# A hybrid DeltaNet / sparse-attention layer: constants loaded first, gate rows kept in DRAM, and the last down-projection unit swept token tile by token tile

## The chip, the cores and the metric

The kernel runs on one core of one Trainium2 chip. The metric is the device time of one execution in microseconds (us). The kernel before takes 3674.93 us, the median of three runs (3673.78, 3674.93, 3680.48). Its profile comes from one further execution, which took 3680.55 us.

## The reference, cut to what matters

One inference step of a one-layer decoder on a prompt of 2048 tokens and on 8 single-token samples, all in float32, width 1024, feed-forward width 2816:

```python
mod = silu(c) @ w_ada + b_ada                  # six parts of 1024: shift, scale, gate, twice
h = rmsnorm(x, g_norm) * (1 + scale1) + shift1
p = h @ w_in                                   # columns for both head groups
o = concat(gated_deltanet(p), sparse_attention(p))
x = x + gate1 * (o @ w_out)
h = rmsnorm(x, g_norm2) * (1 + scale2) + shift2
a = silu(h @ w1) * (h @ w3)                    # w_ffn_in
x = x + gate2 * (a @ w_ffn_out)
y = rmsnorm(x, g_final)
```

The names in this excerpt are shortened; the outputs also hold the new keys, values, indexer keys, convolution rows and DeltaNet states. What the change touches is `mod`, the two gated additions, and the last line.

## The kernel before, in words

**Arithmetic.** A float32 product is made from three passes of TensorE: both operands are split into a rounded high part and a rest, and `mm3` (lines 178 to 182) issues high by high, high by low, low by high. Every 128x512 weight tile is therefore cast on ACT (L163) and subtracted on DVE (L164) before TensorE can use it.

**Stages.** The prompt is worked in 4 groups (g = 0 to 3) of 512 tokens, each of 4 token tiles (t = 0 to 3) of 128. First come the constants (L245 to L291), the modulation (L294 to L367) and, group by group, the normalisation of the input, the projections `w_in` and the DeltaNet chain. The second stage runs the sparse attention (index scores L1626, softmax, `PT` x `V` at L1688), the eight samples, and per group `ffn(g)` (L1751 to L1994): `w_out`, a gated addition, the second normalisation, `w_ffn_in` in 11 pairs, two pairs to a unit (the last unit has one pair), and after each unit's pairs its share of `w_ffn_out`, here called the down projection, in two column halves `hf`. A last unit has two weight tiles per half. The sums of one half stand in the four PSUM banks `d`, one for each token tile.

**The start.** SyncE (SP) issues nearly all loads from one queue, in program order. The vectors come first, then parts 0 and 1 of `w_ada`, eight 512 KB pieces each, into tiles that are borrowed from later work (hh, hl, qk, kq, ct, wi; L314 to L316), then the rest of the constants `cf` (L329) and `cr` (L330), then the first group's input `xt` (2 MB, `load_x`, L435 and L626), then the weights `wsr` and `wr` of `w_in`. `modulate(part)` takes 512 columns at a time: 8 products of a `w_ada` tile with the conditioning (L351), a copy out of PSUM on ACT (L353), then 16 small products with the selection matrix `f4` (L358), which is part of `cf`, and the addition of the bias on DVE (L360). `xt` is squared on ACT (L375). The first product of the projections is L180 with the normalised input `hh` (cast at L414).

**Gate rows.** The two gated additions need the gate along the free axis, the same in all partitions. `rowb(base)` (L1728 to L1739) makes it: for each half 4 transposes of a broadcast column of `mod` (L1735, base 16 or 40) into a `g` bank, and one ACT copy (L1737). It is called twice in each group, before `w_out` and before `w_ffn_in`. The tile `row` has two buffers, and `g_final` is loaded into one of them too (L1983).

**The gated addition.** `gated_add` (L1766) multiplies a bank by `row` on DVE (L1769) into `tm` for t < 2 and into `ca` for t >= 2, and adds the product to `xt` (L1770), on DVE where its argument `soon` is set, else on GpSimd (POOL). Only the second half of the last unit has `soon` in the down projection.

**The order of the work.** Several generators run in turns under a planner (`weave`, `step`, L491 to L529). Each yields an estimated TensorE time, waits and the PSUM tags that it uses or needs. The planner keeps a model of when a PSUM slot comes free and switches to attention pieces whenever their share is due. So the order of the instructions is fixed when the program is built, and a yield that goes missing shifts which attention piece falls beside which part of `ffn`. The tag `g` is shared by `rowb` and the attention output.

**The end.** In the last group the samples' part of each weight tile (16 products with 32 columns, L1812) is issued beside the prompt's. After the last unit the queue of side work is emptied (`tick(True)`, L1981), `g_final` is loaded, and each token tile is closed: `rnorm` (L382 on DVE, the power on POOL at L383), the scaling (L1986, DVE), the output DMA (L1987). The samples' row comes last (L1993, L1994). A second copy of attention and feed-forward stands behind a branch at L1543 that this input doesn't take.

Of the kernel before, what the change touches and what calls it, by code (L numbers as in the profile page):

```python
# [25 lines left out]
F32 = mybir.dt.float32  # L26
# [10 lines left out]
D = 1024  # L37
# [18 lines left out]
RB = 2  # L56
# [56 lines left out]
class K:  # L113
# [102 lines left out]
    def build(self):  # L216
        tc, nc = self.tc, self.nc
        with ExitStack() as es:
# [12 lines left out]
            self.vp_d = self.dr.tile([NS, 128, NPAGE, 256], F32, name="vp_d")  # L231
            self.x2_d = self.dr.tile([T, D], F32, name="x2_d")
# [61 lines left out]
    def modulation(self):  # L294
# [18 lines left out]
        self.ada = [st[i::2] for i in range(2)]  # L313
        for part in range(2):  # L314
            for k in range(KB):
                nc.sync.dma_start(self.ada[part][k], A["w_ada"][0, k * 128:(k + 1) * 128, part * D:(part + 1) * D])  # L316
# [12 lines left out]
        nc.sync.dma_start(self.cf[:, 128:], A["cf"][:, 128:NC0])  # L329
# [100 lines left out]
    def phase1(self, es):  # L430
# [4 lines left out]
        self.x0 = self.load_x(0)  # L435
# [145 lines left out]
    def projects(self):  # L581
        nxt = None
        for g in range(self.ng):
# [15 lines left out]
            for said in extra:  # L599
                yield said[0], said[1]  # L600
        yield lambda: not self.queue
# [1126 lines left out]
    def rowb(self, base):  # L1728

        nc, p = self.nc, self.p  # L1730
        row = p.tile([128, D], F32, name="row", tag="row", bufs=RB)
        for a in range(2):
            pt = self.ps.tile([128, 512], F32, name="g", tag="g", bufs=2)
            for k in range(4):
                self.o(nc.tensor.transpose(pt[:, k * 128:(k + 1) * 128],  # L1735
                                    self.mod[:, base + a * 4 + k, 0:1].to_broadcast([128, 128]), self.id))
            nc.scalar.copy(row[:, a * 512:(a + 1) * 512], pt)  # L1737
            yield TP, 0, dict(act=0.6, use="g", need=None if a else "g")
        return row  # L1739
# [11 lines left out]
    def ffn(self, g):  # L1751
# [8 lines left out]
        def P(tag):  # L1760
            return self.ps.tile([128, 512], F32, name=tag, tag=tag, bufs=2)
# [53 lines left out]
        def after(gap, cost, run):  # L1815
            side.append((gap, run, cost))
# [23 lines left out]
        yield 0, 0, dict(need="g")  # L1840
        row = yield from self.rowb(16)
# [32 lines left out]
        yield 0, 0, dict(need="g")  # L1874
        row = yield from self.rowb(40)
# [10 lines left out]
        if samp:  # L1886
# [16 lines left out]
            after(1, 0, lambda: None)  # L1903
        np_ = FF // 256
        ms = self.msq()
        per = 2
        for p0 in range(0, np_, per):
# [52 lines left out]
            for hf in range(2):  # L1960
                cs = slice(hf * 512, (hf + 1) * 512)
                pd = D4()
                pq = P("g") if samp else None
                for b in range(nf):
                    fr = (p0 * 2 + b) * 128
                    wh, wl, wr = weights([A["w_ffn_out"][0, fr:fr + 128, cs]])
                    if samp:
                        beside(pq, ax[:, b, :], wr, b == 0, b == nf - 1)
                    yield from three(pd, lambda t: ah[b][:, S(t)], lambda t: al[b][:, S(t)], wh, wl, b, nf - 1)
                last = p0 + per >= np_  # L1970
                for t in range(4):
                    gated_add(pd[t], row[:, cs], xt[:, t, cs], last and hf, t)
                    if last:
                        self.squares(ms[:, t, hf:hf + 1], xt[:, t, cs])
                if samp:
# [6 lines left out]
        gf = p.tile([128, D], F32, name="row", tag="row", bufs=RB)  # L1982
        nc.sync.dma_start(gf, bass.AP(tensor=A["g_final"].tensor, offset=A["g_final"].offset, ap=[[0, 128], [1, D]]))  # L1983
        for t in range(4):
            r = self.rnorm(ms[:, t:t + 1])
            nc.vector.scalar_tensor_tensor(xt[:, t, :], xt[:, t, :], r, gf, op0=OP.mult, op1=OP.mult)  # L1986
            nc.sync.dma_start(O[0][0, g * GT + t * 128:g * GT + (t + 1) * 128], xt[:, t, :])  # L1987
        if samp:
            r = mean(ms)
            gv = gf.rearrange("p (h j c) -> p h j c", h=2, j=4)  # L1990
# [27 lines left out]
```

## Time and profile before

| | |
|---|---|
| median of three runs | 3674.93 us |
| profiled execution | 3680.55 us, span 3678.6 us |
| mean granted clock of TensorE | 0.965 |
| PE (matmul), PEld (weight load) | 3429.4 us (93%), 2649.0 us (72%) |
| DVE, ACT, POOL | 2090.6 us (57%), 1475.8 us (40%), 599.2 us (16%) |
| read from and written to HBM | 435.49 MB, 124.75 MB |

The profiled execution is 5.6 us above the median and beside the slowest of the three runs. A row of the timeline gives the start, the duration, the engine, the line, the operation with output and input tiles, and in brackets how long the engine had stood idle and what released it. A row of the chain of waits gives the start, the length and the work that the end was waiting for then. In the windows view each row is a stretch of time with the busy time of each engine, the granted clock of TensorE (PEclk), the share of the DMA engines and GB/s.

### The profile page before, as it was taken

Reading aid. Unit: us, or ns where it says so; the run is one execution under the profiler, and the core shown is the slowest. Engines: PE = TensorE matmul, PEld = TensorE weight load, DVE = VectorE, ACT = ScalarE, POOL = GpSimd, SP = SyncE. Lnnn points to the kernel's source line nnn. Section 1 sums busy time; section 2 is a strip of 40 time slices with the busy share of each in tenths; the row PEclk is TensorE's granted clock in tenths of the full one; section 3 lists DMA queues with packets and bytes.
Section 4 is the critical chain, followed back from the end, with each engine's and each line's share of the span. In section 5 each row is a group of like instructions: output and inputs, shape, how many; then the busy total and the mean of one; then the engine's idle time right before and its main releaser. Section 6 shows DMA issues by size and latency. Waiting matters only on the chain.

```text
span 3678.6 us, 62998 instructions
## 1 busy us (share of the span) xinstructions
PE 3429.4 (93%) x23441; PEld 2649.0 (72%) x23441; DVE 2090.6 (57%) x4377; ACT 1475.8 (40%) x2868; POOL 599.2 (16%) x548
## 2 busy tenths in 40 slices
PE   7999999999998898999888999999899999899997
PEld 5867778777776776777665677787677777677775
DVE  3656646646644665666667555667666664443434
ACT  3333323323334333344456544564645543322222
POOL 0001000101001023212210122212022112221213
PEclk7999999999999898999998999999999999899998
DMA  6755575575676225455544453335433233432221
GB/s 246 244 204 164 180 243 175 184 241 167 193 262 205 70 94 157 124 167 161 158 153 130 127 174 113 114 98 177 138 91 99 90 103 107 169 107 80 78 82 64
DMA packets 412270, 545.52 MB, mean 148 GB/s; under 512 B 47364, under 2 KB 285225, under 8 KB 411946
## 3 DMA queue, kind: packets, MB, share of 16 engines
q1 hardware_dynamic: 411954, 541.41, 46.2%
q8 instruction: 186, 3.05, 0.3%
q14 instruction: 130, 1.06, 0.1%
HBM read 435.49 MB, written 124.75 MB: 152 GB/s over the span
## 4 chain that ended last, share of the span: by engine, by line
PE 74%; DVE 9%; DMA 7%; ACT 4%; issue 4%; SPq 1%; POOL 0%; DVEq 0%; ACTq 0%; POOLq 0%
PE d L180 18%; PE d L182 16%; PE d L181 16%; PE s L1626 3%; PE g L1688 3%; PE s L1671 2%; DVE wi L164 1%; PE g L1700 1%; DMA wi<-kept 1%; PE g L1812 1%; DMA wr<-in_w_ffn_out_dram 1%; DMA x_d<-xt 1%; PE g L1058 1%; ACT bias L1500 1%; ACT wi L163 1%
## 5 line engine op out<-in xcount | busy, mean ns | idle before, releaser
L180 PE MATMUL d<-hh,wi 128*128 128x512 f32 x1792 | 778.8, 435 | 24.0 <-DVE tm L1769 5.8
L181 PE MATMUL d<-hl,wi 128*128 128x512 f32 x1792 | 710.6, 397 | 7.0 <-DVE hl L415 5.8
L182 PE MATMUL d<-hh,wi 128*128 128x512 f32 x1792 | 710.6, 397 | 0.0
L164 DVE TENSOR_TENSOR wi<-wr,wi 128x512 fp32r<-128x512 f32 x537 | 402.7, 750 | 470.1 <-ACT wi L163 467.4
L163 ACT CAST wi<-wr 128x512 fp32r<-128x512 f32 x537 | 332.3, 619 | 784.5 <-PE d L182 499.2
L180 PEld LDWEIGHTS d<-hh,wi 128*128 128x128 f32 x1792 | 342.0, 191 | 120.9 <-issue 29.4
L182 PEld LDWEIGHTS d<-hh,wi 128*128 128x128 f32 x1792 | 341.6, 191 | 77.8 <-DVE wi L164 0.8
L181 PEld LDWEIGHTS d<-hl,wi 128*128 128x128 f32 x1792 | 343.1, 191 | 75.6 <-DVE hl L415 10.6
L180 PE MATMUL d<-wi,hh 128*128 128x512 f32 x768 | 324.7, 423 | 20.5 <-DMA wi<-kept 13.2
L180 PE MATMUL d<-wi,ah 128*128 128x512 f32 x704 | 301.2, 428 | 8.8 <-ACT ah L1940 5.6
L181 PE MATMUL d<-wi,hh 128*128 128x512 f32 x768 | 302.0, 393 | 1.0 <-DVE wi L164 1.0
L182 PE MATMUL d<-wi,hl 128*128 128x512 f32 x768 | 302.4, 394 | 0.0
L182 PE MATMUL d<-wi,al 128*128 128x512 f32 x704 | 282.2, 401 | 3.2 <-POOL al L1941 2.6
L181 PE MATMUL d<-wi,ah 128*128 128x512 f32 x704 | 282.2, 401 | 0.0
L1941 POOL TENSOR_TENSOR al<-ca,ah 128x512 fp32r<-128x512 f32 x88 | 119.1, 1365 | 844.9 <-ACT ah L1940 608.4
L1635 DVE SCALAR_TENSOR_TENSOR sc<-rl,iw,sc 128x512 f32<-128x512 f32 (+3 forms) x224 | 165.8, 740 | 81.5 <-ACT rl L1628 75.5
L1628 ACT ACTIVATE rl<-s 128x512 f32<-128x512 f32 (+3 forms) x288 | 150.3, 544 | 144.1 <-PE s L1626 136.6
L1770 POOL TENSOR_TENSOR xt<-xt,tm 128x512 f32<-128x512 f32 x96 | 136.5, 1436 | 411.5 <-DVE tm L1769 365.7
L180 PEld LDWEIGHTS d<-wi,hh 128*128 128x128 f32 x768 | 145.2, 189 | 68.7 <-DMA wi<-kept 17.0
L1626 PE MATMUL s<-ik,iqT 128*128 128x512 f32 (+3 forms) x576 | 170.8, 396 | 10.0 <-ACT rl L1628 9.7
L1500 ACT ACTIVATE bias<-sc,sv 128x640 bf16<-128x640 f32 (+11 forms) x120 | 169.7, 1414 | 22.8 <-DVE sv L1502 13.5
L180 PEld LDWEIGHTS d<-wi,ah 128*128 128x128 f32 x704 | 135.2, 192 | 52.6 <-issue 11.0
(532 smaller groups left out, 5587.5 us busy)
## 6 DMA issues: line engine op xcount, KB each, us to landing
wi<-kept SPq DMA_DIRECT2D x168, 512.0 KB, 3.4
wr<-in_w_ffn_in_dram SPq DMA_DIRECT2D x572, 128.0 KB, 2.3
wr<-in_w_ffn_out_dram SPq DMA_DIRECT2D x143, 256.0 KB, 2.6
kept<-wi SPq DMA_DIRECT2D x56, 512.0 KB, 3.4
xt<-in_x_prompt_dram SPq DMA_DIRECT2D x8, 2048.0 KB
row<-in_w_ada_dram SPq DMA_DIRECT2D x32, 512.0 KB, 4.3
wr<-in_w_in_dram SPq DMA_DIRECT2D x56, 256.0 KB, 3.6
kT<-kT_d SPq DMA_DIRECT2D x54, 256.0 KB, 3.0
```

The costliest lines, as they stand in the source:

```text
L163: nc.scalar.copy(w[:, 0], wr)
L164: nc.vector.tensor_tensor(w[:, 1], wr, w[:, 0].bitcast(F32), op=OP.subtract)
L180: self.o(nc.tensor.matmul(out, wh, xh, start=start, stop=False, **kw))
L181: self.o(nc.tensor.matmul(out, wh, xl, start=False, stop=False, **kw))
L182: self.o(nc.tensor.matmul(out, wl, xh, start=False, stop=stop, **kw))
L1500: nc.scalar.activation(c, s, AF.Sign, bias=t, accum_out=cnt)
L1626: self.o(nc.tensor.matmul(ps[:, :w], iq[:, h, :].bitcast(F32R), B["ikT"][c * 2 + a][:, :w].bitcast(F32R), start=a == 0, stop=a == 1))
L1628: nc.scalar.activation(r[:, :w], ps[:, :w], AF.Relu)
L1635: nc.vector.scalar_tensor_tensor(s, r[:, :w], iw, s, op0=OP.mult, op1=OP.add)
L1688: self.o(nc.tensor.matmul(po[:, :256], V[:, kb % 4, :], PT[:, b * 256:(b + 1) * 256], start=kb == 0, stop=kb == i))
L1770: (nc.vector if soon else nc.gpsimd).tensor_tensor(xt, xt, tm, op=OP.add)
L1941: nc.gpsimd.tensor_tensor(al[b], a, ah[b].bitcast(F32), op=OP.subtract)
```

## The change

Three parts, independent in the text:

1. The load of `cf` is issued ahead of `w_ada`, and the load of the first group's `xt` between `w_ada` part 0 and part 1. `cr` keeps its place behind part 1.
2. The gate column of `mod` is copied on DVE after projections g = 1 (base 16) and g = 3 (base 40) and written to DRAM, 1024 elements of 4 bytes. `rowb` is then one DMA that reads this row into all partitions (512 KB), on SP's queue. Its transposes, its ACT copies and its three kinds of yields are gone.
3. The second half of the last group's last down unit keeps both weight tiles and sweeps t by t: all six products of a token tile, then its gated addition, its squares and its close. In all groups the close stands in the loop over the token tiles, and `g_final` is loaded by the first close.

```diff
+        nc.sync.dma_start(self.cf[:, 128:], A["cf"][:, 128:NC0])
         for part in range(2):
+            if part:
+                self.x0 = self.load_x(0)
             for k in range(KB):
                 nc.sync.dma_start(self.ada[part][k], A["w_ada"][0, k * 128:(k + 1) * 128, part * D:(part + 1) * D])
...
-        nc.sync.dma_start(self.cf[:, 128:], A["cf"][:, 128:NC0])
         nc.sync.dma_start(self.cr, A["cf"][:, NC0:])
...
-        self.x0 = self.load_x(0)
...
+            for base in {1: (16,), 3: (40,)}.get(g, ()):
+                nc = self.nc
+                col = self.m("gate")
+                nc.vector.tensor_copy(col[:, 0:8], self.mod[:, base:base + 8, 0])
+                nc.sync.dma_start(self.gates[base].rearrange("(m c) -> c m", c=128), col[:, 0:8])
...
     def rowb(self, base):
-        for a in range(2):
-            pt = self.ps.tile([128, 512], F32, name="g", tag="g", bufs=2)
-            for k in range(4):
-                self.o(nc.tensor.transpose(pt[:, k * 128:(k + 1) * 128],
-                                    self.mod[:, base + a * 4 + k, 0:1].to_broadcast([128, 128]), self.id))
-            nc.scalar.copy(row[:, a * 512:(a + 1) * 512], pt)
-            yield TP, 0, dict(act=0.6, use="g", need=None if a else "g")
+        row = self.p.tile([128, D], F32, name="row", tag="row", bufs=RB)
+        g = self.gates[base]
+        self.nc.sync.dma_start(row, bass.AP(tensor=g.tensor, offset=g.offset, ap=[[0, 128], [1, D]]))
         return row
...
-        yield 0, 0, dict(need="g")
-        row = yield from self.rowb(16)
+        row = self.rowb(16)
...
+        def close(t):
+            if not gf:
+                gf.append(p.tile([128, D], F32, name="row", tag="row", bufs=RB))
+                nc.sync.dma_start(gf[0], bass.AP(tensor=A["g_final"].tensor, offset=A["g_final"].offset, ap=[[0, 128], [1, D]]))
+            r = self.rnorm(ms[:, t:t + 1])
+            nc.vector.scalar_tensor_tensor(xt[:, t, :], xt[:, t, :], r, gf[0], op0=OP.mult, op1=OP.mult)
+            nc.sync.dma_start(O[0][0, g * GT + t * 128:g * GT + (t + 1) * 128], xt[:, t, :])
+
+        def finish(t, pd):
+            cs = slice(512, 1024)
+            gated_add(pd, row[:, cs], xt[:, t, cs], True, t)
+            self.squares(ms[:, t, 1:2], xt[:, t, cs])
+            close(t)
...
+                    if samp and hf and last:
+                        kept.append((wh, wl))
+                    else:
+                        yield from three(pd, lambda t: ah[b][:, S(t)], lambda t: al[b][:, S(t)], wh, wl, b, nf - 1)
+                for t in range(4 if kept else 0):
+                    for b, w in enumerate(kept):
+                        self.mm3(pd[t], ah[b][:, S(t)], al[b][:, S(t)], *w, b == 0, b == nf - 1)
+                        yield 3 * MM, 0, bank(t, b, nf - 1)
+                    finish(t, pd[t])
+                if kept:
+                    self.done += nf
+                for t in range(0 if kept else 4):
                     gated_add(pd[t], row[:, cs], xt[:, t, cs], last and hf, t)
                     if last:
                         self.squares(ms[:, t, hf:hf + 1], xt[:, t, cs])
+                    if last and hf:
+                        close(t)
```

**What moves at the start.** SP's queue at the start of the program, before: the second part of `w_ada` (hl to wi), then the constants, then the input of group 0 (xt).

```order
L316 DMA hl<-in_w_ada_dram 128x1024 x4
L316 DMA qk<-in_w_ada_dram 128x1024
L316 DMA kq<-in_w_ada_dram 128x1024
L316 DMA ct<-in_w_ada_dram 128x1024
L316 DMA wi<-in_w_ada_dram 128x1024
L329 DMA cf<-in_cf_dram 128x482
L330 DMA cr<-in_cf_dram 128x1224
L626 DMA xt<-in_x_prompt_dram 128x4x1024
L442 DMA al<-in_a_log_dram 128x4
```

The same queue now, from the constants on to the second part of `w_ada`:

```order
L315 DMA cf<-in_cf_dram 128x482
L320 DMA hh<-in_w_ada_dram 128x1024 x4
L320 DMA qk<-in_w_ada_dram 128x1024
L320 DMA kq<-in_w_ada_dram 128x1024
L320 DMA ct<-in_w_ada_dram 128x1024
L320 DMA wi<-in_w_ada_dram 128x1024
L633 DMA xt<-in_x_prompt_dram 128x4x1024
L320 DMA hl<-in_w_ada_dram 128x1024 x4
```

`cf` has moved ahead of sixteen pieces, and `xt` ahead of eight of them; what follows `cr` keeps its order.

ACT's queue at the same place, before: squares of `xt` (L375), casts of the first input weights (L163) and the copies out of the modulation's banks (L353; 257 and 264 are those of part 1's first half, 281 and 288 those of its second).

```order
L163 CAST wi<-wr 128x512
L375 ACTIVATE junk,msq<-xt 128x512
L163 CAST wi<-wr 128x512
L375 ACTIVATE junk,msq<-xt 128x512
L353 COPY m_257<-s 128x512
L375 ACTIVATE junk,msq<-xt 128x512
L353 COPY m_264<-s 128x512
L375 ACTIVATE junk,msq<-row 8x512 x2
L353 COPY m_281<-s 128x512
L353 COPY m_288<-s 128x512
L163 CAST wi<-wr 128x512
```

Now, with the same copies under the numbers 259, 266, 283 and 290:

```order
L378 ACTIVATE junk,msq<-xt 128x512 x5
L356 COPY m_259<-s 128x512
L356 COPY m_266<-s 128x512
L447 ACTIVATE nA<-al 128x4
L459 CAST wsh<-wsr 128x320 x2
L378 ACTIVATE junk,msq<-row 8x512 x2
L163 CAST wi<-wr 128x512
L356 COPY m_283<-s 128x512
L163 CAST wi<-wr 128x512
L356 COPY m_290<-s 128x512
L854 COPY raw<-hist 128x3 x4
L163 CAST wi<-wr 128x512
```

All squares of `xt` now precede part 1's first copies, and two casts of input weights stand ahead of its last copy.

**What moves between group 0 and group 1.** TensorE's queue behind the last down product of group 0, before (L1626 index scores, L1671 attention scores; ik numbers name key blocks):

```order
L182 MATMUL d<-wi,al 128x512
L1626 MATMUL s<-ik_15047,iqT 128x512
L1626 MATMUL s<-ik_15049,iqT 128x512
L1671 MATMUL s<-kT,qT 128x512
L1626 MATMUL s<-ik_15047,iqT 128x512
L1626 MATMUL s<-ik_15049,iqT 128x512
L1626 MATMUL s<-ik_15051,iqT 128x128
L1626 MATMUL s<-ik_15053,iqT 128x128
```

The same place now (L1633 is the old L1626, L1707 the old L1700 that transposes probabilities, L1695 the old L1688):

```order
L182 MATMUL d<-wi,al 128x512
L1707 MATMUL g<-cf,big 128x128 x4
L1695 MATMUL g<-PT,V 128x256 x2
L1633 MATMUL s<-ik_15047,iqT 128x512
L1633 MATMUL s<-ik_15049,iqT 128x512
L1707 MATMUL g<-cf,big 128x128 x4
L1695 MATMUL g<-PT,V 128x256 x2
L1633 MATMUL s<-ik_15047,iqT 128x512
L1633 MATMUL s<-ik_15049,iqT 128x512
L1633 MATMUL s<-ik_15051,iqT 128x512
```

An earlier piece of attention now falls behind the last down product: from there to the first `w_out` product of group 1 the queue holds 88 products, where it held 56 with the 8 transposes of `rowb`. Among the last 48 down products of group 0 stand 18 attention products now, 54 before.

**What moves at the end.** DVE's queue in the last unit of group 3, before (banks 36107 to 36110 are t = 0 to 3 of the second half):

```order
L1769 TENSOR_TENSOR tm_36092<-d_36040,row_32582 128x512
L1769 TENSOR_TENSOR ca_36169<-d_36109,row_32582 128x512
L1769 TENSOR_TENSOR ca_36174<-d_36110,row_32582 128x512
L1770 TENSOR_TENSOR xt_32128<-xt_32128,ca_36169 128x512
L1769 TENSOR_TENSOR tm_36154<-g_36043,sc_32153 128x128
L1769 TENSOR_TENSOR tm_36159<-d_36107,row_32582 128x512
L1770 TENSOR_TENSOR xt_32128<-xt_32128,ca_36174 128x512
L1541 TENSOR_SCALAR again_36241<-g_36239 1x1
L1769 TENSOR_TENSOR tm_36164<-d_36108,row_32582 128x512
L1770 TENSOR_TENSOR xt_32128<-xt_32128,tm_36159 128x512
L1770 TENSOR_TENSOR xt_32128<-xt_32128,tm_36164 128x512
L1769 TENSOR_TENSOR tm_36187<-g_36111,sc_32153 128x128
```

The same place now (banks 36027 to 36030 are t = 0 to 3; L1770 and L1771 are the old L1769 and L1770):

```order
L1770 TENSOR_TENSOR tm_36012<-d_35960,row_32513 128x512
L1770 TENSOR_TENSOR tm_36048<-d_36027,row_32513 128x512
L1771 TENSOR_TENSOR xt_32070<-xt_32070,tm_36048 128x512
L1770 TENSOR_TENSOR tm_36067<-d_36028,row_32513 128x512
L1771 TENSOR_TENSOR xt_32070<-xt_32070,tm_36067 128x512
L1770 TENSOR_TENSOR ca_36084<-d_36029,row_32513 128x512
L1771 TENSOR_TENSOR xt_32070<-xt_32070,ca_36084 128x512
L1770 TENSOR_TENSOR ca_36101<-d_36030,row_32513 128x512
L1770 TENSOR_TENSOR tm_36120<-g_35963,sc_32084 128x128
L1771 TENSOR_TENSOR xt_32070<-xt_32070,ca_36101 128x512
L1770 TENSOR_TENSOR tm_36133<-g_36031,sc_32084 128x128
L385 SCALAR_TENSOR_TENSOR rny4_36055<-msq_32536 128x1
```

The token tiles are now taken in the order 0, 1, 2, 3, each multiplied and added before the next; before, tiles 2 and 3 came first. The closes follow behind all four, as before.

More of the change, by code (lines that the diff above doesn't have):

```diff
@@ L231, in build @@
             self.vp_d = self.dr.tile([NS, 128, NPAGE, 256], F32, name="vp_d")
+            self.gates = {b: self.dr.tile([D], F32, name=f"gate{b}") for b in (16, 40)}
             self.x2_d = self.dr.tile([T, D], F32, name="x2_d")
@@ L1728, in rowb @@
     def rowb(self, base):
-        nc, p = self.nc, self.p
-        row = p.tile([128, D], F32, name="row", tag="row", bufs=RB)
-        for a in range(2):
-            pt = self.ps.tile([128, 512], F32, name="g", tag="g", bufs=2)
-            for k in range(4):
-                self.o(nc.tensor.transpose(pt[:, k * 128:(k + 1) * 128],
-                                    self.mod[:, base + a * 4 + k, 0:1].to_broadcast([128, 128]), self.id))
-            nc.scalar.copy(row[:, a * 512:(a + 1) * 512], pt)
-            yield TP, 0, dict(act=0.6, use="g", need=None if a else "g")
+        row = self.p.tile([128, D], F32, name="row", tag="row", bufs=RB)
+        g = self.gates[base]
+        self.nc.sync.dma_start(row, bass.AP(tensor=g.tensor, offset=g.offset, ap=[[0, 128], [1, D]]))
         return row
@@ L1873, in ffn @@
         self.scale_rows(xt, ms, True)
-        yield 0, 0, dict(need="g")
-        row = yield from self.rowb(40)
+        row = self.rowb(40)
         yield 0, 20, dict(act=3, dve=4, need="s")
@@ L1903, in ffn @@
             after(1, 0, lambda: None)
+        gf = []
+        def close(t):
[10 more added lines that the diff above has]
+            close(t)
         np_ = FF // 256
@@ L1963, in ffn @@
                 pq = P("g") if samp else None
+                last, kept = p0 + per >= np_, []
                 for b in range(nf):
@@ L1968, in ffn @@
                         beside(pq, ax[:, b, :], wr, b == 0, b == nf - 1)
-                    yield from three(pd, lambda t: ah[b][:, S(t)], lambda t: al[b][:, S(t)], wh, wl, b, nf - 1)
-                last = p0 + per >= np_
-                for t in range(4):
+                    if samp and hf and last:
[10 more added lines that the diff above has]
+                for t in range(0 if kept else 4):
                     gated_add(pd[t], row[:, cs], xt[:, t, cs], last and hf, t)
@@ L1981, in ffn @@
         yield from tick(True)
[L1982 to L1987, printed above, removed]
         if samp:
             r = mean(ms)
-            gv = gf.rearrange("p (h j c) -> p h j c", h=2, j=4)
+            gv = gf[0].rearrange("p (h j c) -> p h j c", h=2, j=4)
             for j in range(4):
```

## The prediction

> **What bounds the kernel now.** I read the page first, then the chain of waits, then the timelines of the three places that the change touches. The page's chain says by engine what the end waited for:
>
> ```profile
> PE 74%; DVE 9%; DMA 7%; ACT 4%; issue 4%; SPq 1%; POOL 0%; DVEq 0%; ACTq 0%; POOLq 0%
> ```
>
> TensorE is the bound over nearly the whole span, so time is to be had in two ways: take products off its queue, or close the gaps in which it stands. The largest gap is at the start. The chain of waits from 0 to 62 us, up to the first projection product:
>
> ```profile
> 17.98 9.62 DMA cf<-in_cf_dram
> 27.75 3.60 PE s L358 x16
> ...
> 55.46 0.79 PE d L180
> ```
>
> The chain runs through the load of `cf`, which stands in the queue behind all of `w_ada`. TensorE's timeline shows the wait that this makes: the last product with part 0, then nothing until `cf` is there.
>
> ```profile
> 16.73 1.05 PE L351 MATMUL s<-wi,cT 128*32 128x512 f32 x2 [0.22 <-DMA wi<-in_w_ada_dram]
> 27.75 3.60 PE L358 MATMUL s<-cf,m 128*128 128x32 f32 x16 [9.97 <-DMA cf<-in_cf_dram]
> 38.74 1.94 PE L351 MATMUL s<-hl,cT 128*32 128x512 f32 x8
> ```
>
> **Part 1, the start.** What the load costs is read from the queue: SP issues as fast as the ring takes pieces, and the DMA view has their sizes.
>
> ```profile
> 16.70 0.33 SPq L316 DMA_DIRECT2D wi<-in_w_ada_dram  x1
> 17.98 0.33 SPq L329 DMA_DIRECT2D cf<-in_cf_dram  x1
> 42.58 0.38 SPq L162 DMA_DIRECT2D wr<-in_w_in_dram  x1
> ```
>
> ```profile
> hh<-in_w_ada_dram SPq DMA_DIRECT2D x4, 512.0 KB
> xt<-in_x_prompt_dram SPq DMA_DIRECT2D x1, 2048.0 KB
> cf<-in_cf_dram SPq DMA_DIRECT2D x1, 241.0 KB
> ```
>
> One 512 KB piece takes 17.98 - 16.70 = 1.28 us. `cf` ahead of part 0 costs 241/512 x 1.28 = 0.60 us: the product that began at 16.73 begins at 17.33. What follows is on ACT:
>
> ```profile
> 17.82 0.58 ACT L353 COPY m<-s 128x512 f32<-128x512 f32 x1 [3.86 <-PE s L351]
> ...
> 40.67 0.60 ACT L163 CAST wi<-wr 128x512 fp32r<-128x512 f32 x1
> ...
> 50.34 0.59 ACT L353 COPY m<-s 128x512 f32<-128x512 f32 x1 [1.12 <-PE s L351]
> ...
> 53.88 0.24 ACT L189 CAST hs<-ca 128x64 fp32r<-128x64 f32 x1 [2.06 <-DVE ca L426]
> ```
>
> The copy that ended at 17.82 + 0.58 = 18.40 ends at 19.00, and L358 can start there and not at 27.75: 8.75 us earlier. Three things could be late next. First, part 1 now comes behind 2048 KB of `xt`, which cost 4 x 1.28 = 5.12 us. Before, its last piece had landed by 27.1 (the end of `cf`'s wait, 27.75, less `cf`'s own 0.60), so now by 27.1 + 0.60 + 5.12 = 32.8. With everything 8.75 us earlier the first half of part 1 starts at 38.74 - 8.75 = 30.0, needs that piece in its second bank, some 1.9 us later, and loses about 1 us at most. The wait is so nearly covered, but without the slack that it had. Second, ACT's order: part 1's last copy now stands behind two casts of input weights. What the queue holds ahead of those weights is the same in sum, so they land as before; the second cast ran without a wait at 40.67 and so ends by 41.3, while the copy is due at 50.34 - 8.75 = 41.6. Third, a third cast now stands ahead of `hs` and the first `hh`; its weights were issued at 42.58, behind a store that follows the first cast's DVE step. `hs` is due at 53.88 - 8.75 = 45.1. If that load keeps its time and needs 3 us, its cast ends at 46.2 or later and 1 to 2 us are given back; I expect it earlier, since DVE reaches that step earlier. The squares of `xt` no longer stand between part 1's copies on ACT, which gives some tenths back. I take -8.5 us for the start, with -6.5 and -9.97 (the whole wait) as ends. From the first projection product on TensorE sets the pace, and the gain is carried to the end.
>
> **Part 2, the gate rows.** The answer for the transposes, and TensorE's idle time at their lines:
>
> ```profile
> L1735 PE MATMUL g<-cf,mod x64: 270/273/323, 1161.1 to 3199.2; 128*128 128x128 f32 x64
> ...
>   ACT row L1737: 3.8, 4
>   ACT PT L1716: 1.7, 3
> ```
>
> ```profile
> 3142.07 1.03 PE L1735 MATMUL g<-cf,mod 128*128 128x128 f32 x8
> 3142.86 0.48 PE L180 MATMUL d<-wi,hh 128*128 128x512 f32 x1
> 3208.47 1.14 PE L411 MATMUL s<-cf,xt 128*128 128x128 f32 x3 [9.04 <-DVE xt L404]
> ```
>
> Eight transposes hold TensorE for 3142.86 - 3142.07 = 0.79 us, so the eight calls hold 6.3 us, and up to 5.5 us of waits stand at them. Not all of it is on the path: the second call of each group comes just before TensorE waits for the normalised input anyway, 9.04 us in the last group, so there it is worth nothing. The four first calls count in full, 3.2 us, and some of the waits; I take -4, with 0 and -8 as ends. ACT loses 16 copies, which nothing waits for but the next product. Added are eight row loads, two DVE copies and two gate stores on SP's queue. The nearest load in the trace is that of `g_final`, with the same shape:
>
> ```profile
> L1983 SPq DMA_DIRECT2D row<-in_g_final_dram x4: 327/330/497, 1225.4 to 3228.2; - x4
> ...
> DMA to landing us min/median/max: 5.7/5.7/5.7
> ```
>
> It holds SP 0.33 us and lands after 5.7. The row is first read when half of `w_out` is done, 96 products of 0.23 or 22 us after its first, so the landing is covered. If SP has to wait for a free `row` buffer, or for the gate store of base 40, which stands two places ahead of group 0's read of it, then the `oT` loads and the next weights are queued behind; I count that as 0 with +3 as the end, and without cover a call would cost the 5.7. The gate stores write 4-byte elements, and no row shows such a store's cost by itself.
>
> The planner moves too. The stretches that hold the last down products of group 0, and then attention alone up to group 1's first `w_out` product:
>
> ```profile
> 1817.30:1844.20 26.90, 26.26 (x113) 20.64 (x114) 19.80 (x29) 16.98 (x36) 9.44 (x8) 0.94 0.45 142
> 1844.20:1873.70 29.50, 17.55 (x67) 11.67 (x65) 19.70 (x55) 18.00 (x37) 2.63 (x4) 0.71 0.66 234
> ```
>
> ```profile
> PE s L1626 <- ACT rl L1628: 6.7, 6, 2.1
> ```
>
> In the first, 48 down products at 0.23 us (the pace in part 3's rows) leave 15.7 us for 54 attention products, 0.29 each; 36 of them leave it now, 10.5 us. The second takes 29.5 us for 56 products, 0.53 each, and gets 32 more: 9.3 us at 0.29, 17.0 at 0.53. The net is -1 to +7; I take +2, near the lower end, since the piece that moves in is independent of the 6.7 us of waits for ACT and can fill them.
>
> **Part 3, the sweep.** The end in the chain of waits, on DVE and on POOL:
>
> ```profile
> 3652.28 0.23 PE d L182
> ...
> 3657.01 0.24 PE d L182
> 3657.35 0.66 DVE ca L1769
> ```
>
> ```profile
> 3661.32 1.27 DVE L1770 TENSOR_TENSOR xt<-xt,tm 128x512 f32<-128x512 f32 x2
> ...
> 3663.94 1.28 DVE L1986 SCALAR_TENSOR_TENSOR xt<-xt,rnz,row 128x1024 f32<-128x1024 f32 x1 [0.18 <-POOL rnz L383]
> ...
> 3669.91 2.01 DVE L1993 SCALAR_TENSOR_TENSOR sc<-sc,rnz,row 8x256 f32<-8x256 f32 x4 [0.44 <-POOL rnz L383]
> ```
>
> ```profile
> 3654.27 1.28 POOL L1770 TENSOR_TENSOR xt<-xt,tm 128x512 f32<-128x512 f32 x1
> ...
> 3663.35 1.06 POOL L383 TENSOR_TENSOR rnz<-rny,mhalf 128x1 f32<-128x1 f32 x2
> ...
> 3668.42 1.45 POOL L383 TENSOR_TENSOR rnz<-rny,mhalf 128x1 f32<-128x1 f32 x1 [1.03 <-DVE rny L382]
> ```
>
> DVE's first step of the second half is at 3657.35, and the last of the eight ends at 3661.32 + 1.27 = 3662.6; the closes start 1.3 later. Swept by tile, the six products of a tile take 6 x 0.23 = 1.4, so t = 0 is full three tiles, 4.2 us, before the sweep's end at about 3657.3: at 3653. Its two steps run beside the products. t = 1 needs the `tm` that POOL frees at 3654.27 + 1.28 = 3655.55; from there DVE has six steps of 0.66 and two short ones of the samples, to about 3660. With the same 1.3 the closes start near 3661, 2.9 earlier, and the rest of the chain (four closes, the samples' row) is as long as before, less a few tenths, since the samples' steps no longer stand between the tiles. A power that takes 0.53 alone takes 1.45 beside a close, which stays so. I take -3.3, with 0 (a chain through ACT's squares and POOL holds it) and -6.5 (all eight steps hidden) as ends. The page "SBUF — State Buffer" of the Trainium skill ("Who interferes with whom") says that a DVE instruction with two SBUF inputs and a GpSimd one that reads SBUF exclude each other; by it the added DVE steps beside POOL's adds would cost one add, an estimate of 1.3, and the end would gain 2.0. The powers' 1.45 beside a close agree with it; no row shows it for the adds.
>
> **The sum.** -8.5 - 4 + 2 - 3.3 = -13.8 us. On the profiled execution that is 3680.55 - 13.8 = 3666.7; that execution lay 5.6 above the median, so the forecast is 3674.93 - 13.8 = 3661.1, rounded to 3661. The forecast's own range, with half of each part's ends, is 3655 to 3668.
>
> **The rivals.** *The clock comes up too.* The windows of the start show the granted clock in the last column but two:
>
> ```profile
> 4.00:17.80 13.80, 10.37 (x25) 2.41 (x25) 1.49 (x2) 2.24 (x4) 0.61 (x3) 1.00 0.96 364
> ...
> 27.70:31.30 3.60, 3.56 (x20) 3.52 (x21) 0.00 (x0) 0.00 (x0) 0.70 (x2) 0.50 1.02 409
> ...
> 55.40:60.80 5.40, 5.34 (x15) 4.14 (x15) 1.43 (x3) 0.62 (x2) 0.00 (x0) 0.50 0.28 99
> ```
>
> It is 1.00 before the wait and 0.50 after it, still so when the projections begin. If the shorter wait keeps it at 1.00, the modulation itself gains little, since the loads bind it next, but the first 5.4 us of projections take 2.7: 3661.1 - 2.7 = 3658. The page "TensorE: Matmul & The Clock Gate" (Part 1) says that an idle window of about 3.4 us halves the clock and a busy one restores it; the trace agrees with the first, but at 27.70 to 31.30 TensorE is busy for 3.56 of 3.60 us and stays at 0.50, so I give it 0.12.
>
> *The start is given back and the rows were hidden.* The third input weight is late as worked out above, -6.5, and `rowb` always ran where TensorE waited, 0: -6.5 + 2 - 3.3 = -7.8 at most, and with the planner's upper half -5: 3667 to 3670, no change that a measurement can tell. For it: ACT's new order, and the 5.5 us of waits at the transposes. Against: the 3142.07 row runs without a gap into `w_out`. A case of this kind is also that a part does not do what it says, such as a sweep that is still closed last. 0.22.
>
> *Slower: attention alone between group 0 and group 1.* TensorE's granted clock is 0.71 there. If the 32 added products come at the stretch's own pace and the longer idle brings the clock to the 0.50 seen at the start, the 17.55 us busy become 24.9, the stretch 36.9 us for 56 products, 0.66 each, and 88 take 58 us: 28.5 more. If the down stretch stays at its 26.9 because DVE and ACT set it, the sum is -8.5 - 4 - 3.3 + 28.5 = +12.7: 3688. It decides from a stretch of 29.5 + 15.8 + 7.3 = 52.6 us on. Against: the same attention work is done in sum. 0.08.
>
> **How the numbers follow.** The forecast has 0.58, the rivals 0.12, 0.22 and 0.08. About 0.2%, 7.3 us, is what a measurement of this kernel can tell from no change. The forecast and the clock are faster by more: 0.70; the second rival is the same: 0.22; the third slower: 0.08. The range takes the clock case with the lower ends of the rows, the sweep and the planner, 3648, and the whole second rival with some of its spread, 3673.
>
> **What would show it.** Right: L358 begins near 19 and the first L180 near 47; no transposes before `w_out`; the stretch from group 0's last down product to group 1's `w_out` below 40 us; DVE's first close near 3661 less the gain before it. Wrong: a new wait of L351 or `hh` for a load near 33 to 46; SP rows of several microseconds at a row load with weights queued behind; a stretch above 50 us; a DVE that idles between token tiles at the end.

## The result, and the profile after

The changed kernel takes 3648.10 us (median of 5 runs, 3645.45 to 3654.75), the kernel before beside it 3673.78 (median of 5, 3669.31 to 3680.48): a ratio of 0.9930, 95% interval [0.9916, 0.9944], 25.7 us faster. The forecast was 3661, 13.8 us faster, with a range of 3648 to 3673. Its direction held. Its size was half of what came, and the experiments show that nearly all of the gain came from the order of the instructions, a part that the forecast had put at 2 us to the bad. Of all executions of the experiments below one, of the kernel without the yields of base 40, took 15414.99 us; it is left out of that kernel's numbers.

The two profiled executions differ by more, 3678.6 to 3643.7 us of span. Executions of one kernel spread over 10 to 20 us here, the profiled one before lay high and the one after low, so the traces show places, and the amounts are taken from the medians and the ratios. Places in a trace are given by the products of L180, counted from 0: every kernel here has 3304 of them. An attention product is one of L1626, L1671, L1688, L1700 or L1714, under the numbers of the kernel before.

**The start.** TensorE's timeline of the changed kernel, from the first products with `f4` (L361, the old L358) to the first projection product:

```profile
18.47 0.41 PE L361 MATMUL s<-cf,m 128*128 128x32 f32 x2
...
20.53 1.93 PE L361 MATMUL s<-cf,m 128*128 128x32 f32 x14 [0.68 <-ACT m L356]
...
34.13 1.05 PE L354 MATMUL s<-wi,cT 128*32 128x512 f32 x2 [0.24 <-DMA wi<-in_w_ada_dram]
...
41.47 0.41 PE L361 MATMUL s<-cf,m 128*128 128x32 f32 x2 [2.02 <-ACT m L356]
...
49.94 0.79 PE L180 MATMUL d<-hh,wi 128*128 128x512 f32 x1 [0.70 <-ACT hh L417]
```

The wait of 9.97 us is gone and L361 starts near 19, as worked out. But the first projection product is at 49.94, not near 47: 5.5 us earlier than before. ACT's rows say what came late next:

```profile
37.35 0.95 ACT L459 CAST wsh<-wsr 128x320 fp32r<-128x320 f32 x2 [1.16 <-DMA wsr<-in_w_in_dram]
38.96 0.63 ACT L378 ACTIVATE junk<-row 8x512 f32<-8x512 f32 x1 [0.67 <-DMA row<-in_x_sample_dram]
...
41.85 0.57 ACT L356 COPY m<-s 128x512 f32<-128x512 f32 x1
...
45.77 0.62 ACT L163 CAST wi<-wr 128x512 fp32r<-128x512 f32 x1 [2.97 <-DMA wr<-in_w_in_dram]
48.16 0.24 ACT L189 CAST hs<-ca 128x64 fp32r<-128x64 f32 x1 [1.78 <-DVE ca L429]
```

ACT's rows stand in the order of its queue. The loads of `wsr`, the sample rows and the input weights are no earlier than before (SP issues the sample rows at 36.35, before at 34.81, and the first input weights at 36.70, before at 35.16), and ACT waits for them ahead of part 1's last copies and, 2.97 us, ahead of `hs` and `hh`. The chain of waits has it in one line of descent: the sample rows, their squares, the first cast, its store, and the load of the third weight that is issued behind that store.

```profile
36.35 2.52 DMA row<-in_x_sample_dram
38.96 0.73 ACT junk L378 x2
...
42.13 3.62 DMA wr<-in_w_in_dram
45.77 0.63 ACT wi L163
```

**Between the groups.** The windows of the three stretches around group 1's `w_out` (its products are left out): from group 0's last down product to `w_out`, from `w_out`'s last product to the first of `w_ffn_in`, and the first pairs of `w_ffn_in` with the attention beside them. Before:

```profile
1843.60:1873.70 30.10, 18.15 (x70) 12.18 (x68) 20.30 (x56) 18.56 (x39) 2.63 (x4) 0.72 0.66 231
1937.90:1975.80 37.90, 28.35 (x119) 18.33 (x118) 23.94 (x75) 30.89 (x58) 2.32 (x3) 0.82 0.53 172
1975.80:2038.00 62.20, 54.15 (x237) 43.02 (x236) 45.62 (x92) 28.55 (x51) 3.28 (x3) 0.95 0.35 109
```

After:

```profile
1825.80:1867.40 41.60, 30.35 (x111) 19.24 (x110) 29.19 (x73) 27.48 (x56) 4.62 (x5) 0.84 0.64 216
1931.30:1952.30 21.00, 13.61 (x69) 10.24 (x68) 18.48 (x49) 18.25 (x38) 1.39 (x2) 0.92 0.55 192
1952.30:2015.00 62.70, 58.94 (x272) 45.97 (x271) 50.89 (x121) 40.28 (x72) 4.05 (x4) 1.00 0.42 130
```

The first stretch grew by 11.5 us, as forecast. The second, which the prediction did not price, shrank by 16.9: an attention piece that stood alone between `w_out` and `w_ffn_in` now runs later, beside the first products of `w_ffn_in`. Counted in the traces, 624 attention products are done when `w_out` begins, in both kernels; when `w_ffn_in` begins it is 754 before and 724 now. So the third stretch takes 35 more products and is nearly as long, at a granted clock of 1.00 and not 0.95. TensorE's waits show what the old second and third stretch were made of:

```profile
1955.06 0.60 PE L1714 MATMUL g<-cf,st 128*128 128x128 f32 x2 [2.96 <-ACT row L1737]
1964.73 0.33 PE L1700 MATMUL g<-cf,big 128*128 128x128 f32 x1 [2.33 <-ACT big L1679]
1967.32 1.76 PE L1700 MATMUL g<-cf,big 128*128 128x128 f32 x7 [2.25 <-ACT big L1679]
...
2004.35 0.80 PE L181 MATMUL d<-hl,wi 128*128 128x512 f32 x1 [2.77 <-DVE hl L415]
2014.84 0.50 PE L180 MATMUL d<-hh,wi 128*128 128x512 f32 x1 [2.41 <-DVE th L1935]
```

**The end.** DVE and POOL in the last unit of the changed kernel (L1770 and L1771 are the multiply and the add, L1910 the close):

```profile
3622.63 0.84 DVE L1771 TENSOR_TENSOR xt<-xt,tm 128x512 f32<-128x512 f32 x1
...
3624.29 0.87 DVE L1771 TENSOR_TENSOR xt<-xt,tm 128x512 f32<-128x512 f32 x1
...
3627.81 0.28 DVE L1770 TENSOR_TENSOR tm<-g,sc 128x128 f32<-128x128 f32 x1
...
3629.32 1.28 DVE L1910 SCALAR_TENSOR_TENSOR xt<-xt,rnz,row 128x1024 f32<-128x1024 f32 x1
...
3635.29 2.00 DVE L2014 SCALAR_TENSOR_TENSOR sc<-sc,rnz,row 8x256 f32<-8x256 f32 x4 [0.44 <-POOL rnz L386]
```

```profile
3622.88 1.74 POOL L1771 TENSOR_TENSOR xt<-xt,tm 128x512 f32<-128x512 f32 x1
...
3633.80 1.45 POOL L386 TENSOR_TENSOR rnz<-rny,mhalf 128x1 f32<-128x1 f32 x1 [1.03 <-DVE rny L385]
```

The gated steps end at 3627.81 + 0.28 = 3628.1, the closes start 1.2 later and the rest of the chain is as long as before. From the samples' row to the end it is 8.4 us (3643.7 - 3635.29) and was 8.7 (3678.6 - 3669.91).

### The profile page after: what moved, and what is told of

Same layout as the page of the kernel before. It is cut to its first block, busy times and chain, and to the rows that moved or that the text cites. A ratio compares the mean times of both kernels' runs of the same rounds, so it can differ in the third digit from the quotient of the medians.

```text
span 3643.7 us, 62857 instructions
## 1 busy us (share of the span) xinstructions
PE 3414.4 (94%) x23377; PEld 2634.8 (72%) x23377; DVE 2087.8 (57%) x4379; ACT 1469.1 (40%) x2852; POOL 599.0 (16%) x548
## 3 DMA queue, kind: packets, MB, share of 16 engines
q8 instruction: 186, 3.05, 0.3%
## 4 chain that ended last, share of the span: by engine, by line
PE 74%; DVE 9%; DMA 7%; ACT 5%; issue 4%; SPq 1%; POOL 0%; DVEq 0%; ACTq 0%; POOLq 0%
PE d L180 19%; PE d L182 17%; PE d L181 17%; PE s L1633 3%; PE g L1695 2%; PE s L1678 2%; DMA wi<-kept 2%; DVE wi L164 1%; PE g L1813 1%; PE g L1707 1%; ACT bias L1507 1%; PE g L1065 1%; DMA wr<-in_w_ffn_out_dram 1%; ACT wi L163 1%; DMA xt<-in_x_prompt_dram 1%
## 5 line engine op out<-in xcount | busy, mean ns | idle before, releaser
L180 PE MATMUL d<-hh,wi 128*128 128x512 f32 x1792 | 780.8, 436 | 25.4 <-DVE tm L1770 8.2
L163 ACT CAST wi<-wr 128x512 fp32r<-128x512 f32 x537 | 331.9, 619 | 792.5 <-PE d L182 507.6
L180 PEld LDWEIGHTS d<-hh,wi 128*128 128x128 f32 x1792 | 342.3, 191 | 125.2 <-issue 26.5
L180 PE MATMUL d<-wi,hh 128*128 128x512 f32 x768 | 326.2, 425 | 18.0 <-DMA wi<-kept 12.9
L180 PE MATMUL d<-wi,ah 128*128 128x512 f32 x704 | 301.4, 428 | 11.8 <-DVE th L1950 5.9
L1771 POOL TENSOR_TENSOR xt<-xt,tm 128x512 f32<-128x512 f32 x96 | 137.2, 1444 | 425.1 <-DVE tm L1770 368.6
L180 PEld LDWEIGHTS d<-wi,hh 128*128 128x128 f32 x768 | 145.3, 189 | 68.5 <-DMA wi<-kept 16.8
L1633 PE MATMUL s<-ik,iqT 128*128 128x512 f32 (+3 forms) x576 | 171.2, 395 | 10.2 <-ACT rl L1635 9.8
L180 PEld LDWEIGHTS d<-wi,ah 128*128 128x128 f32 x704 | 133.5, 190 | 57.8 <-issue 13.8
```

What stands on the lines that cost most here:

```text
L163: nc.scalar.copy(w[:, 0], wr)
L180: self.o(nc.tensor.matmul(out, wh, xh, start=start, stop=False, **kw))
L1633: self.o(nc.tensor.matmul(ps[:, :w], iq[:, h, :].bitcast(F32R), B["ikT"][c * 2 + a][:, :w].bitcast(F32R), start=a == 0, stop=a == 1))
L1771: (nc.vector if soon else nc.gpsimd).tensor_tensor(xt, xt, tm, op=OP.add)
```

## The experiments

Each part was run alone, then the planner's order was separated from the transposes, then the order was moved without touching either. The kernel before was timed beside each set of runs; its medians there were 3674.75, 3674.48 and 3674.71.

**The gate rows alone**, part 2 of the change in full, on the kernel before:

```diff
-        yield 0, 0, dict(need="g")
-        row = yield from self.rowb(16)
+        row = self.rowb(16)
...
-        yield 0, 0, dict(need="g")
-        row = yield from self.rowb(40)
+        row = self.rowb(40)
```

with the new `rowb` and the two gate stores.

> The gate rows read from DRAM alone, with the planner's yields gone, and nothing else of the change. The traces of the two full kernels put most of the gain (15 to 20 us of 35 between those two executions) into group 1 between its w_out and its second down projection, and 4 more at the same place of group 2. Both theories of that place want this kernel 14 to 18 us faster than before: theory A, the new order of attention pieces, theory B, the transposes and their ACT copies that are gone. If the gain was only a difference of two executions: 2 us faster, as the prediction had it (-4 and +2).

3651.36 us, ratio 0.9949 [0.9930, 0.9968]: 23.4 us faster by the medians, 18.7 by the ratio. Most of the gain is in this part, where the forecast had 2.

**The rows from DRAM in the old order.** The transposes and copies are gone, their yields are kept:

```diff
+        row = self.p.tile([128, D], F32, name="row", tag="row", bufs=RB)
+        g = self.gates[base]
+        self.nc.sync.dma_start(row, bass.AP(tensor=g.tensor, offset=g.offset, ap=[[0, 128], [1, D]]))
         for a in range(2):
-            pt = self.ps.tile([128, 512], F32, name="g", tag="g", bufs=2)
-            for k in range(4):
-                self.o(nc.tensor.transpose(pt[:, k * 128:(k + 1) * 128],
-                                    self.mod[:, base + a * 4 + k, 0:1].to_broadcast([128, 128]), self.id))
-            nc.scalar.copy(row[:, a * 512:(a + 1) * 512], pt)
             yield TP, 0, dict(act=0.6, use="g", need=None if a else "g")
```

> The gate rows read from DRAM, but rowb still yields its two transposes' time and the g slot to the planner, so that every instruction except the transposes and copies keeps the order of before. Theory A (order): 3 to 5 us faster, no more than the transposes' own time. Theory B (transposes and copies were on the path): 12 to 16 us faster, nearly all of e1_rows, with the 2.96 us wait for the copy of a row in group 1 gone.

3675.91 us, ratio 1.0003 [0.9992, 1.0015]: no change that can be measured. The transposes and copies that go and the row loads and gate stores that come are together worth between -3 and +5.5 us. Theory B falls. The sum hides a loss, which is shown below under the rows. The second stretch and the waits in it, in this kernel:

```profile
1940.90:1975.20 34.30, 25.95 (x112) 16.96 (x111) 23.42 (x73) 28.43 (x54) 2.32 (x3) 0.80 0.59 190
```

```profile
1959.82 0.70 PE L1677 MATMUL s<-kT,qT 128*128 128x512 f32 x1 [2.16 <-DVE st L1678]
1964.62 0.47 PE L1706 MATMUL g<-cf,big 128*128 128x128 f32 x1 [2.03 <-ACT big L1685]
1966.99 1.75 PE L1706 MATMUL g<-cf,big 128*128 128x128 f32 x7 [1.90 <-ACT big L1685]
```

The wait of 2.96 for the copy of a row is gone, and one of 2.16 for the softmax on DVE stands in its place: the copy had only been the last of several that the attention piece waited for. Some of it is gone all the same: the stretch takes 34.3 us here, and 35.6 to 37.9 in the four other traces of this order.

**The old transposes in the new order.** Only the yields are dropped:

```diff
             nc.scalar.copy(row[:, a * 512:(a + 1) * 512], pt)
-            yield TP, 0, dict(act=0.6, use="g", need=None if a else "g")
...
-        yield 0, 0, dict(need="g")
-        row = yield from self.rowb(16)
+        row = self.rowb(16)
```

and the same for base 40.

> The converse: transposes and ACT copies as before, only the yields of rowb are gone, so that all other instructions have the order of the changed kernel. Theory A (order): 10 to 14 us faster, and the attention stretch of group 1 without its waits. Theory B: no change, within 2 us.

3650.56 us, ratio 0.9943 [0.9923, 0.9963]: 24.2 us faster by the medians, 20.9 by the ratio (14 to 28), with every transpose still there. Theory A holds, and by more than the 10 to 14 it expected; the lower end of the interval touches them. The second stretch is as short as in the changed kernel:

```profile
1930.20:1951.80 21.60, 15.08 (x78) 11.37 (x77) 18.49 (x49) 18.01 (x39) 1.39 (x2) 0.92 0.51 183
```

**The start alone**, part 1 of the change on the kernel before:

```diff
+        nc.sync.dma_start(self.cf[:, 128:], A["cf"][:, 128:NC0])
         for part in range(2):
+            if part:
+                self.x0 = self.load_x(0)
...
-        nc.sync.dma_start(self.cf[:, 128:], A["cf"][:, 128:NC0])
...
-        self.x0 = self.load_x(0)
```

> The start alone: constants first, input of group 0 between the parts of w_ada. The trace of the changed kernel has the first projection product at 49.94 and not at 55.46, so this kernel should be 5.5 us faster if the gain is kept to the end, 4.4 if the loads behind the start give some back. The prediction had 8.5.

3671.97 us, ratio 0.9995 [0.9983, 1.0006]: 1.8 us by the ratio, which can't be told from nothing; its interval reaches to -6.2. The first projection product is at 50.60, so the start itself is 4.9 earlier than in the profile of before. That is beyond the spread: the four traces with the new start have this product at 49.50 to 50.60, the ten others at 52.83 to 57.91.

**The sweep alone**, part 3 on the kernel before, with `close` and `finish` as in the change:

```diff
+                for t in range(4 if kept else 0):
+                    for b, w in enumerate(kept):
+                        self.mm3(pd[t], ah[b][:, S(t)], al[b][:, S(t)], *w, b == 0, b == nf - 1)
+                        yield 3 * MM, 0, bank(t, b, nf - 1)
+                    finish(t, pd[t])
```

> The sweep of the last unit and the closes inside the loop, alone. The order up to the last unit is that of before. In the trace of the changed kernel the end lay 3.8 us closer behind the last unit's start than before, so 3.3 to 3.8 us faster, if nothing ahead of it moves; the prediction had 3.3. The stretch from the last w_out of group 3 on has no planner choice left, so it should be the same in both.

3672.11 us, ratio 0.9995 [0.9982, 1.0007]: not to be told from no change, interval from -6.6 to +2.6. What the traces show of it is below.

**The constants alone first.** The load of `cf` moves, the input of group 0 doesn't:

```diff
+        nc.sync.dma_start(self.cf[:, 128:], A["cf"][:, 128:NC0])
         for part in range(2):
...
-        nc.sync.dma_start(self.cf[:, 128:], A["cf"][:, 128:NC0])
```

> Only the load of cf moved to the front; the input of group 0 stays behind both parts of w_ada and behind cr. If the loads behind part 1 (the casts of input weights on ACT, which wait for them) set the first projection product, it comes at 50 to 53 as in the changed kernel and the gain is again 2 to 5 us. If it was the 2 MB of input between the parts that cost the rest of the forecast 8.5, it comes at 47 or earlier and the gain is 8.

3673.21 us, ratio 1.0005 [0.9994, 1.0016]: no change. The first projection product is at 53.17:

```profile
53.17 0.79 PE L180 MATMUL d<-hh,wi 128*128 128x512 f32 x1 [0.70 <-ACT hh L414]
```

```profile
36.06 0.63 ACT L375 ACTIVATE junk<-xt 128x512 f32<-128x512 f32 x1 [5.84 <-DMA xt<-in_x_prompt_dram]
...
47.44 0.62 ACT L163 CAST wi<-wr 128x512 fp32r<-128x512 f32 x1 [1.34 <-DMA wr<-in_w_in_dram]
```

This lies within the spread of the kernels with the old start. So the 2 MB between the parts did not cost the rest of the forecast; without them ACT waits 5.84 us for the input. Both orders of the loads that were run end at a load that ACT needs next.

**One call's yields.** As in the run of the old transposes in the new order, but for base 16 only, and for base 40 only:

```diff
+            if base == 40:
                 yield TP, 0, dict(act=0.6, use="g", need=None if a else "g")
...
-        yield 0, 0, dict(need="g")
         row = yield from self.rowb(16)
```

> Transposes and copies as before; only the yields of the first row of each group (base 16, ahead of w_out) are gone. Theory A1, the order between the groups carries the gain: 15 to 24 us faster. Theory A2, the order between w_out and w_ffn_in carries it: within 5 us of before. Theory A3, any shift of the attention pieces gives another draw: any number, but not the sum with the next run.

> As the run before, but only the yields of the second row (base 40, between w_out and w_ffn_in) are gone. Theory A1: within 5 us of before. Theory A2: 15 to 24 us faster. Theory A3: any number.

Base 16 alone: 3665.88 us, ratio 0.9972 [0.9960, 0.9985], 10.3 us. Base 40 alone: 3670.74 us, ratio 0.9988 [0.9975, 1.0002], 4.4 us, just not clear of noise. Neither place carries it alone (A1 and A2 fall). The two add up to 14.7 us by the ratios, less than the 20.9 of both together, but with these intervals the difference isn't clear of noise, so A3's "not the sum" is not shown. With either set of yields gone the second stretch shrinks, to 22.0 and 20.2 us. But with base 40 alone the piece that left it costs later in group 1: between the 1680th and the 2080th L180 product that trace has 508 attention products, before 476, and from the 1720th to the 2080th that kernel takes 378.3 us, before 362.9, the changed kernel 359.2.

**The planner's pace.** One constant, on the kernel before and on the changed one, both ways:

```diff
-MM, TP, F4, LAG, EARLY, PACE, GONE_BY = 0.23, 0.46, 0.88, 0.6, 3000, 463, 1e9
+MM, TP, F4, LAG, EARLY, PACE, GONE_BY = 0.23, 0.46, 0.88, 0.6, 3000, 455, 1e9
```

> The kernel before, with one constant of the planner moved by under 2% (PACE 463 to 455), so that attention pieces come earlier; no instruction is added or taken away. Theory A3 (the order is a draw, and before's order was an unlucky one at group 1's w_ffn_in): the time moves by 5 to 25 us, either way. Rival (only the missing yields matter, the rest of the order is worth little): within 4 us of before.

> The same constant moved the other way (463 to 471), attention pieces later. Theory A3: 5 to 25 us, either way. Rival: within 4 us of before.

> The changed kernel with PACE 455. Theory A3: it leaves its 3648 by 5 us or more, more likely upward, since a draw that gained 24 us is a good one; if it falls further, it is the better kernel. Rival (the change keeps its gain under any order): 3644 to 3652.

> The changed kernel with PACE 471. Theory A3: it leaves its 3648 by 5 us or more. Rival: 3644 to 3652.

| PACE | kernel before | changed kernel |
|---|---|---|
| 455 | 3679.32, 1.0017 [1.0008, 1.0026] | 3655.73, 0.9948 [0.9935, 0.9961] |
| 463 | 3673.78 | 3648.10, 0.9930 [0.9916, 0.9944] |
| 471 | 3698.07, 1.0060 [1.0047, 1.0073] | 3654.12, 0.9946 [0.9933, 0.9959] |

Ratios are to the kernel before at 463. A constant that adds no instruction moves the kernel before by 0.17% and 0.60%, some 6 and 22 us: theory A3 holds in that, and 471 decides it, since the interval at 455 reaches into the 4 us of its rival. On the changed kernel both settings lie some 6 us higher, but the intervals overlap with that at 463. And a draw is not the whole truth: at each of the three settings the changed kernel is faster, by 24, 26 and 44 us of the medians. The kernel before was no unlucky draw among its neighbours; both neighbours are slower. The second stretch is the same at both other settings (36.2 and 35.8 us with the yields, 21.7 and 21.4 without), so that shortening comes with the yields and not with the draw. The same holds of the later pairs of group 0, from the 1200th to the 1512th L180 product: 324.6 and 325.0 us with the yields, 315.4 and 319.2 without. What else differs is in later stretches and goes with the setting. No version run here has a lower median than the changed kernel; the two with all yields gone on the kernel before, 3651.36 and 3650.56, can't be told from it.

## Why the prediction came out as it did

**What bounds the kernel** held: TensorE in its order, 94% busy after. So did the sign.

**The step that failed is the planner's term, +2.** It measured the down stretch and the attention stretch behind it, got the second one's growth right (9.3 to 17.0 forecast, 11.5 seen), and stopped there. For these two stretches +2 was right: from the 1512th to the 1528th L180 product the five traces in the old order take 54.8 to 56.6 us, the three in the new order 57.4 to 59.4. Every other stretch was put at nothing without a reason. The one between `w_out` and `w_ffn_in` of group 1 takes 34.3 to 37.9 us in the five and 21.0 to 21.6 in the three, some 15 less. The later pairs of group 0, from the 1200th to the 1512th, take 320.8 to 328.0 and 315.6 to 318.5, some 7 less; the order changes there too, from the 1127th product on. Measured by itself with the transposes kept, the order is worth -24.2 us by the medians and -20.9 by the ratio, with an interval of [0.9923, 0.9963]. I had the order of both kernels and the trace of before with its waits there, and had looked at the second stretch only for the transposes.

Two counts in that term are off, though the +2 does not hang on them. The traces have 66 products between group 0's last down product and `w_out` before, 8 of them the transposes, and 108 now, where the text counts 56 and 88; among the 48 down products they have 64 and 20 attention products, not 54 and 18. So the eight transposes that leave are in the -4 and are taken off the 32 added products a second time. And 26.9 less 48 products of 0.23 leaves 15.9 us, not 15.7.

**The rows, -4,** were 0: 1.0003 [0.9992, 1.0015], which leaves out -4. That 0 is a gain and a loss. The prediction put the gate stores at 0, since no row showed what such a store costs. Now there is one. The store for base 40 takes 10.57 us to land. SP stands 7.28 us at the row load that reads it, one of the signs that the prediction had named. And its source is one of the eight buffers that ACT's copies `qo` use too; the copy whose turn it is waits for the landing, the softmax behind it on ACT is late, and TensorE waits 4.68 us. After, and the same place before in the last line:

```profile
1140.57 10.57 DMA gate<-gate
...
1151.22 0.59 ACT L959 COPY qo<-s 128x512 f32<-128x512 f32 x1 [3.41 <-DMA gate<-gate]
1152.88 0.90 PE L1707 MATMUL g<-cf,Dm 128*128 128x128 f32 x3 [4.68 <-ACT Dm L1686]
...
1154.83 0.55 PE L1700 MATMUL g<-cf,Dm 128*128 128x128 f32 x3 [1.16 <-ACT Dm L1679]
```

From the 920th to the 940th L180 product the five traces with gate stores take 56.0 to 58.1 us, the nine without 51.5 to 51.8. The store for base 16 lands after 11.61 us, and the stretch around it, from the 460th to the 480th, takes 27.8 to 28.3 against 25.8 to 26.3. So the two stores cost some 6 to 7 us. No run takes them away alone. If that is right, the transposes and copies are worth some 1 to 10 us, an estimate from these rows and the interval above, and the -4 for them may have been right; the term that failed here is the stores' 0.

**The start, -8.5,** was 4.9 to 5.5 at the first projection product and 1.8 on the time, not told from 0. The mechanism stood in the prediction as its third concern: the third cast did wait for its load, 2.97 us. I had expected DVE to release that load early enough. Its cause in turn was shown too: the first cast stood behind squares of the sample rows, whose load had not moved. In the three other traces with the new start that wait is 3.05 to 4.32 us. That the remaining gain fades along the first stage is what the traces suggest: from the first to the 920th L180 product the kernels with the new start take 1057.4 to 1058.2 us, the others 1051.2 to 1060.3. That is no proof.

**The sweep, -3.3.** From the 3280th L180 product to the end of the span it was 43.7 us (3678.6 - 3634.9) and is 39.9 (3643.7 - 3603.8): -3.8. The sweep alone has 40.2 there, and all kernels without it 43.4 to 44.0. The size was right; on the time of the whole it can't be told from nothing. The Trainium skill's page "SBUF — State Buffer" ("Who interferes with whom") has the lock between DVE and GpSimd; the rows bear it out in part, with smaller prices than the 1.3 that I made of it: DVE's adds took 0.84 and 0.87 and not 0.68, POOL's add 1.74 and not 1.28.

**The rivals.** The clock did come up, but not where that rival needed it: in three of its four rounds fourteen products of L361 took 1.75 to 1.93 us, where before sixteen took 3.60 in the first and only the last round ran at 1.75; the loads bound the modulation as said, and the first projections ran at 0.50 as before. The windows:

```profile
35.80:37.50 1.70, 1.65 (x14) 1.64 (x14) 0.31 (x2) 0.36 (x2) 0.00 (x0) 1.00 0.68 148
...
49.90:55.50 5.60, 5.48 (x15) 4.20 (x16) 1.55 (x3) 0.62 (x1) 0.00 (x0) 0.50 0.35 126
```

The second rival, "given back and hidden", was right on the start. The rows came to nothing as it said, but the traces show the stores' loss and not that `rowb` always ran where TensorE waited. Only the order's gain kept the result from it. The slower rival was priced from the right place: the stretch that it watched came to 41.6 us, short of the 52.6 from which it decides.

**The range** held by 0.1 us, and that is luck: the gain came from a term that stood in the sum with the other sign. Its lower end took the planner at -1, 3 us below the +2; the term's real bounds were what an order can do, and that was some 20 us either way (20.9 faster without the yields, 22 slower at a pace of 471).

## What to carry to other kernels

When a change removes yields, costs or instructions that a planner sees, price every stretch whose order changed, not only the one around the edit: count the products between landmarks in both orders, and ask which waits of the old trace lie in a stretch that gets shorter. Then run the order apart from the instructions; keeping the yields and dropping the work, and the reverse, took two kernels and settled it. And a gain at the start of a queue is worth what the next load in that queue allows: follow the in-order engine behind the wait one step further than the step that was freed. Where a run comes to 0, look in its trace for what was added before putting what was taken away at nothing: a small store that lands late holds its source buffer, and whoever takes that buffer next waits.

## What was not expected of the hardware

A store of 1024 elements of 4 bytes took 10.57 and 11.61 us to land, where the load of `wr` above took 3.62.

The granted clock at the start does not follow how busy TensorE is over a few microseconds. In the changed kernel, cut into steps of 3.4 us, it is the same all through a step:

```profile
22.00:25.40 3.40, 3.40 (x19) 0.92 (x18) 0.20 (x1) 1.53 (x4) 0.00 (x0) 0.50 1.03 410
25.40:28.80 3.40, 2.54 (x23) 2.09 (x22) 0.33 (x2) 3.30 (x10) 0.71 (x1) 1.00 1.02 407
28.80:32.20 3.40, 3.40 (x10) 0.36 (x4) 2.15 (x5) 2.27 (x7) 0.71 (x1) 0.50 1.03 412
32.20:35.60 3.40, 2.74 (x9) 0.58 (x8) 0.78 (x2) 0.39 (x1) 0.00 (x0) 1.00 1.01 287
```

Here the steps in which TensorE is busy throughout are those at 0.50, in part because the same products take longer there. The page "TensorE: Matmul & The Clock Gate" of the Trainium skill (Part 1) has the gate decide by a free-running window of about 3.4 us; the steps agree with the window. What in a window decides is not shown: in the kernel before TensorE was busy for 3.40 of 3.40 us from 30.00 to 33.40, and the clock stayed at 0.50.

What stays open: why each order costs what it does in the later stretches. The traces show in which stretches the time goes, but no rule that ranks two orders ahead of a run.
